# In-projection by rows: one pinned weight split instead of many, and a unit's first sums in the quarter before

## The chip, the cores and the metric

The kernel runs on one core of a Trainium2 chip. The metric is the device time of one execution in microseconds (us). The core's engines are PE (TensorE: matmuls, and the weight loads PEld that overlap them), ACT (ScalarE), DVE (VectorE), POOL (GpSimd) and SP (SyncE, which here issues the DMAs). Each engine works through its own instruction queue in order; semaphores order the queues against each other.

## The reference

The reference is one inference step of a two-layer backbone, for 128 context tokens and 128 latent tokens with a model width of 2048. Layer 0 mixes with MLA and grouped-query attention in parallel, layer 1 with differential attention; each layer ends in a gated feed-forward block with a convolution. What matters here is the start of layer 0:

```python
mod = jax.nn.silu(cond) @ w_ada[l] + b_ada[l]
sh1, sc1, gt1, sh2, sc2, gt2 = jnp.split(mod[:, None, :], 6, axis=-1)
h = rmsnorm(x, g_norm_mix[l]) * (1 + sc1) + sh1
...
proj = h @ w_in
```

So before the first projection can start on a block of 128 input features, the shift `sh1` and the scale `sc1` of these features have to be computed from `w_ada`, 2048 rows each. `w_in` is 2048 by 2880.

## The kernel before

**Precision.** A product of two float32 matrices is made from three matmuls in a faster format. Every weight tile is split into a high part `wh` and a low part `wl` (`split`, L225 to L227: ACT copies the tile with rounding, DVE subtracts), the activations `hx` likewise, and a product is `wh*hx_hi + wh*hx_lo + wl*hx_hi`. A DMA brings 16 blocks of 128 by 128 weights (1 MB) into a buffer `raw` (three buffers); a split takes 8 of these blocks, and `wh` and `wl` have four buffers each.

**The in-projection by rows** (`mixer_ab`). Tokens lie on the free axis: all 256 tokens (128 of each group) are one moving operand. There are 16 input blocks k and 23 output columns c. The projection goes in four quarters of four input blocks, so that it can begin when the first block's shift and scale are known. In a quarter the first ten columns ("held", `HELD`) stay in five PSUM banks while the input blocks come one after another (quarter 0: four slices of one block each) or two and two (quarters 1 to 3: two slices); then the other 13 columns follow with all four blocks of the quarter at once (the "free" columns c10 to c22). The result of each quarter is added into SBUF (`leave`).

**The units** (`Early`) give shift and scale. Units 0 to 3 are one input block each, units 4 to 9 two blocks each. A unit has two sums over its weights (`sums(1)` for the scale, from `araw` buffers; `sums(0)` for the shift, from `condb`), 32 small matmuls each, into one PSUM bank `ada`. Then `turn` copies the bank to SBUF on ACT (`am`, L422), `finish` transposes it on PE (L429) and adds up on DVE (L432 to L437), and `modulate` makes the block's `hx` (DVE L589 and L597, ACT L600 and L601, and L584 for the low half, on DVE for even and POOL for odd blocks). `end` is `finish` and `modulate` together. In quarter 0 units 1 to 3 come between the held products; unit 2q+4 comes in the free columns of quarter q, for the first slice of the next quarter, and unit 2q+3 in the first slice of quarter q (1 to 3), for its second slice.

**What sets the order.** The program is planned at compile time: each engine's queue is filled by a planner that takes, by its own estimate of durations, what is ready, earlier traced work first. `keep_in_program_order` pins an instruction behind the one traced before it on its engine. The matmuls of the in-projection are pinned (`product`, until the middle of quarter 3), the sums and transposes of the units too, and in quarter 0 the DMA issues and, through `W.pinned`, the two instructions of each weight split. `W` is a `Stream`: `block` hands out the blocks one by one, and when it has none left it makes the next split from the oldest `raw`. Quarter 0 takes 92 blocks: 40 in the held slices, that is splits 1 to 5, and 52 in the free columns. `W.pinned = False` stands behind the last held slice.

Of the kernel before, what the change touches and what calls it, by code (L numbers as in the profile page):

```python
# [88 lines left out]
def step_kernel(ctx: ExitStack, tc: tile.TileContext, A: dict):  # L89
# [22 lines left out]
    def T_(pl, shape, tag, dt=F32, bufs=None):  # L112
        kw = {} if bufs is None else {"bufs": bufs}
        return pl.tile(shape, dt, tag=tag, name=nm(tag), **kw)
# [84 lines left out]
    def att_bank():  # L199
        return T_(ppool["att"], [P, 512], "att", bufs=3)  # L200
# [24 lines left out]
    def split(out_hi, out_lo, src, pin=lambda i: i):  # L225
        pin(act.copy(out_hi, src))  # L226
        pin(dve.tensor_tensor(out=out_lo, in0=src, in1=out_hi.bitcast(F32), op=ALU.subtract))  # L227
# [72 lines left out]
    class Stream:  # L300
# [15 lines left out]
        def block(self):  # L316
            if not self.blocks:
                if not self.raws:
                    self.fetch()
                raw, n = self.raws[0]  # L320
                m = min(8, n - self.lo)
                wh = T_(wpool, [P, 1024 + P], "wh", F32R, bufs=4)[:, :m * P]
                wl = T_(wpool, [P, 1024 + P], "wl", F32R, bufs=4)[:, :m * P]
                split(wh, wl, raw[:, self.lo * P:(self.lo + m) * P],
                      tc.keep_in_program_order if self.pinned else lambda i: i)
                self.blocks = [(wh[:, b * P:(b + 1) * P], wl[:, b * P:(b + 1) * P]) for b in range(m)]
                self.lo += m
                if self.lo == n:
                    self.raws.pop(0)
                    self.lo = 0  # L330
            return self.blocks.pop(0)
# [146 lines left out]
    def load_row():  # L478
        tc.keep_in_program_order(sp.dma_start(out=condb, in_=A["condb"]))
        for r in range(2):  # L480
            tc.keep_in_program_order(act.activation(condb[:, r], condb[:, r], AF.Silu))
# [237 lines left out]
    def mixer_ab(hx, W, units, st):  # L719
        l = 0  # L720
        with tc.tile_pool(name="ab", bufs=1) as ab:
            with tc.tile_pool(name="abp", bufs=1) as pj:
# [9 lines left out]
                def caches():  # L732
                    tc.keep_in_program_order(sp.dma_start(out=ckc, in_=A["cache_ckv"]))
                    split(kv_in[:, :, 0, T:2 * T], kv_in[:, :, 1, T:2 * T], ckc)
                    for i, half in enumerate(halves):
                        tc.keep_in_program_order(sp.dma_start(out=kr[half, i, T:2 * T], in_=A["cache_krope"][half]))
                    tc.keep_in_program_order(sp.dma_start(out=kg[:, :, T:2 * T], in_=A["cache_gqa_k"]))
                    tc.keep_in_program_order(sp.dma_start(out=vg[:, 1], in_=A["cache_gqa_v"]))
# [81 lines left out]
                def finish(c):  # L820
                    if c < 6:
                        start(queries(c))
                    elif c < 10:
                        start(latents(c - 6))
                    elif c == 10:
                        start(key_rope())
                    elif c < 13:
                        start(keys(c - 11))
                    elif c == 14:
                        start(values(0))  # L830
                    elif c == 15:
                        start(values(1))
# [22 lines left out]
                def product(ps, c, ks, first, last):  # L855
                    pin = (lambda i: i) if free[0] else tc.keep_in_program_order
                    for k in ks:
                        wh, wl = W.block()
                        for n, (w, lo) in enumerate(((wh, 0), (wh, NT), (wl, 0))):
                            pin(pe.matmul(ps, w, hx[:, k, lo:lo + NT], start=first and k == ks[0] and n == 0,  # L860
                                          stop=last and k == ks[-1] and n == 2, skip_group_check=True))

                def leave(c, n, ps, q):
                    to = pr[:, c:c + n] if c < 15 else qb[:, c - 15:c - 15 + n]
                    if q == 0:
                        act.copy(to, ps)
                    else:
                        dve.tensor_tensor(out=to, in0=to, in1=ps, op=ALU.add)

                def held(banks_, ks, q, between, last=False):  # L870
                    first = ks[0] % 4 == 0
                    for c in range(HELD):
                        product(banks_[c // 2][:, c % 2 * NT:(c % 2 + 1) * NT], c, ks, first and c % 2 == 0, last)
                        if last and c % 2:
                            leave(c - 1, 2, banks_[c // 2].rearrange("p (c t) -> p c t", c=2), q)
                            if q == 3:
                                finish(c - 1)
                                finish(c)
                        between(c)

                def at(**steps):
                    return lambda c: [f() for f in steps.get(f"c{c}", ())]

                def scale(u):
                    modulate(hx, rb0, 0, 0, range(u.c0, u.c0 + u.n), held=0 < u.c0 < 4)

                def end(u):
                    u.finish()
                    scale(u)

                scale(units[0])
                for q in range(4):
                    banks_ = [T_(pacc, [P, 512], "acc") for _ in range(3)] + [att_bank() for _ in range(2)]
                    if q == 0:
                        u1, u2, u3 = units[1:4]
                        pin = tc.keep_in_program_order

                        def load(u):
                            u.load(1, pin)
                            u.load(0, pin)  # L900

                        load(u2)
                        u1.sums(1)
                        held(banks_, [0], 0, at(c1=[lambda: u1.sums(0), u1.turn, lambda: load(u3)], c4=[lambda: end(u1)]))
                        W.fetch(pin)
                        u2.sums(1)
                        held(banks_, [1], 0, at(c4=[lambda: u2.sums(0), u2.turn], c6=[lambda: end(u2)]))
                        W.fetch(pin)
                        u3.sums(1)
                        u3.sums(0)  # L910
                        u3.turn()
                        held(banks_, [2], 0, at(c2=[lambda: end(u3)]))
                        held(banks_, [3], 0, at(), True)
                        W.pinned = False
                    else:
                        u = units[2 * q + 3]
                        ks = range(4 * q, 4 * q + 4)
                        held(banks_, ks[:2], q, at(c0=[lambda: u.sums(1)], c2=[lambda: u.sums(0), u.turn],
                                                   c3=[lambda: end(u)]))
                        if q == 3:  # L920
                            free[0] = True
                            pinned[0] = True
                            caches()
                            load_row()
                        held(banks_, ks[2:], q, lambda c: pump(RATE["in3"]) if q == 3 else None, True)
                    if q < 3:
                        u = units[2 * q + 4]
                        u.load(1)
                        u.load(0)
                        steps = at(c13=[lambda: u.sums(1)], c16=[lambda: u.sums(0), u.turn], c17=[lambda: end(u)],  # L930
                                   c18=[lambda: [units[2 * q + 5].load(j) for j in (1, 0)]])
                    else:
                        steps = lambda c: pump(RATE["in3"])
                    for c in range(HELD, NIN):
                        ps = T_(pacc, [P, 512], "acc")[:, :NT]
                        product(ps, c, range(4 * q, 4 * q + 4), True, True)
                        leave(c, 1, ps[:, None, :], q)
                        if q == 3:
                            finish(c)
                        steps(c)  # L940
# [77 lines left out]
        with tc.tile_pool(name="abo", bufs=1) as feat["pool"]:  # L1018
            ensure(l, 2)
            ada["pew"] = PEW["out0"]  # L1020
            W = Weights(A["w_out_ab"], KD, 1)
# [195 lines left out]
    with banks("pab") as ppool["ada"]:  # L1217
# [3 lines left out]
        units = [Early(k, 1) for k in range(4)] + [Early(c, 2) for c in range(4, KD, 2)]  # L1221
        W = Stream(A["w_in_ab"], ([TB] * 5 + [12]) * 4)
# [7 lines left out]
        W = Weights(A["w_up"][0], KD, 1)  # L1230
# [5 lines left out]
    with tc.tile_pool(name="cc", bufs=1) as cp, banks("pc") as ppool["ada"]:  # L1236
        ada["junk"] = lambda: T_(cp, [P, 4, 512], "junk", BF16, bufs=1)
        ppool["att"] = ppool["ada"]
        W = Weights(A["w_in_c"], KD, 1)
# [5 lines left out]
        W = Weights(A["w_up"][1], KD, 1)  # L1245
# [154 lines left out]
```

## Time and profile before

| | before |
|---|---|
| median of 3 runs | 2341.72 us (2340.18 to 2345.34) |
| the profiled execution | 2342.78 us, span 2341.0 us |
| mean granted clock of PE | 0.989 |
| PE busy | 2282.4 us (97%) |
| DVE busy | 1817.4 us (78%) |
| ACT busy | 1178.3 us (50%) |
| first held product starts, first free column starts, quarter 1 starts | 22.0, 63.9 and about 86.5 us |

The span runs from the first to the last instruction; the execution's own time lies 1.8 us around it. PE's busy share counts matmuls at whatever clock was granted, so a matmul at half clock counts double. A row of a timeline gives start, duration, engine, line, operation, what is written from what, the shape, how many instructions are merged, and in brackets the idle time of the engine before it and what ended that. A row of DMA issues ends in the time from issue to landing.

### The profile page before, as it was taken

The page shows a single profiled execution, that of the slowest core. Times are in us where ns is not written, and L with a number is a line of the kernel's source. Part 1 is how long each engine was busy: PE and PEld are TensorE (multiplying, and loading weights), DVE is VectorE, ACT ScalarE, POOL GpSimd, SP SyncE. Part 2 cuts the span into 40 slices and gives each one's busy share as a digit, 9 for nine tenths or more (in the row PEclk, how much of TensorE's full clock was granted, in tenths as well). Part 3 has the DMA queues.
Part 4 walks back from the last instruction along what each step waited for, and adds up shares of the span by engine and source line. Part 5 has one row for each costly group of instructions (what it writes and reads, how often), then busy time and mean ns, then how long its engine had stood idle before and what let it go on. Part 6 is the DMA issues. An engine that isn't in the chain of part 4 may idle for free. (4 is left out here: it accounts for less than half of the span.)

```text
span 2341.0 us, 47384 instructions
## 1 busy us (share of the span) xinstructions
PE 2282.4 (97%) x19806; PEld 2191.6 (94%) x19806; DVE 1817.4 (78%) x2636; ACT 1178.3 (50%) x1865; POOL 149.5 (6%) x133
## 2 busy tenths in 40 slices
PE   5999999999999999999999999999999999999998
PEld 4888878899999999999989999898999999999997
DVE  3566748879999999999969989787899755666654
ACT  2446664465553345554465555446555434555553
POOL 0002101200000000001220000022000000000011
PEclk8999999999999999999999999999999999999999
DMA  8797779867777877777767788786677555555553
GB/s 353 304 359 284 256 294 378 313 255 252 260 263 285 309 263 257 261 264 270 293 237 265 268 325 292 294 317 234 229 260 268 198 196 189 194 197 198 189 192 126
DMA packets 92566, 610.82 MB, mean 261 GB/s; under 512 B 9984, under 2 KB 17856, under 8 KB 20544
## 3 DMA queue, kind: packets, MB, share of 16 engines
q1 hardware_dynamic: 92352, 607.80, 70.5%
q8 instruction: 155, 2.54, 0.4%
q14 instruction: 59, 0.48, 0.1%
HBM read 603.01 MB, written 4.75 MB: 260 GB/s over the span
## 5 line engine op out<-in xcount | busy, mean ns | idle before, releaser
L226 ACT CAST wh<-raw 128x1024 fp32r<-128x1024 f32 (+1 forms) x788 | 792.8, 1012 | 883.2 <-PE acc L377 688.5
L227 DVE TENSOR_TENSOR wl<-raw,wh 128x1024 fp32r<-128x1024 f32 (+1 forms) x788 | 922.6, 1186 | 316.6 <-ACT wh L226 308.4
L376 PE MATMUL acc<-hx,wh 128*128 128x256 f32 x3440 | 952.5, 277 | 1.4 <-ACT wh L226 0.8
L380 PE MATMUL acc<-hx,wl 128*128 128x256 f32 x3440 | 951.5, 277 | 0.2 <-DVE wl L227 0.2
L377 PE MATMUL acc<-hx,wh 128*128 128x256 f32 x3440 | 951.4, 277 | 0.0
L376 PEld LDWEIGHTS acc<-hx,wh 128*128 128x128 f32 x3440 | 646.0, 188 | 7.8 <-issue 5.0
L380 PEld LDWEIGHTS acc<-hx,wl 128*128 128x128 f32 x3440 | 645.6, 188 | 6.4 <-issue 4.2
L377 PEld LDWEIGHTS acc<-hx,wh 128*128 128x128 f32 x3440 | 646.0, 188 | 1.9 <-issue 1.7
L486 DVE CUSTOM_DVE_ANT_0 junk<-araw,condb 128x2048 f32<-128x2048 f32 (+1 forms) x192 | 443.5, 2310 | 0.0
L377 PE MATMUL acc<-g,wh 128*128 128x256 f32 x1408 | 388.3, 276 | 0.0
L380 PE MATMUL acc<-g,wl 128*128 128x256 f32 x1408 | 388.0, 276 | 0.0
L376 PE MATMUL acc<-g,wh 128*128 128x256 f32 x1408 | 387.8, 276 | 0.0
L377 PEld LDWEIGHTS acc<-g,wh 128*128 128x128 f32 x1408 | 264.3, 188 | 0.0
L380 PEld LDWEIGHTS acc<-g,wl 128*128 128x128 f32 x1408 | 264.2, 188 | 0.0
L376 PEld LDWEIGHTS acc<-g,wh 128*128 128x128 f32 x1408 | 264.1, 188 | 0.0
L181 POOL TENSOR_TENSOR sqacc<-sqacc,sq 128x256 f32<-128x256 f32 x62 | 86.2, 1390 | 1576.1 <-issue 1300.0
L860 PE MATMUL acc<-hx,wh 128*128 128x256 f32 x608 | 115.4, 290 | 7.9 <-ACT wh L226 5.6
L860 PEld LDWEIGHTS acc<-hx,wh 128*128 128x128 f32 x608 | 95.6, 194 | 16.3 <-ACT wh L226 6.4
L1169 ACT ACTIVATE cv<-acc,convw 128x256 f32<-128x256 f32 x176 | 98.3, 559 | 1.4 <-PE acc L364 1.4
L650 DVE SCALAR_TENSOR_TENSOR x<-acc,mod,x 128x128 f32<-128x128 f32 x192 | 58.0, 343 | 41.0 <-PE acc L380 40.0
L860 PE MATMUL acc<-hx,wl 128*128 128x256 f32 x304 | 86.7, 286 | 2.2 <-DVE wl L227 2.2
L1172 DVE SCALAR_TENSOR_TENSOR cv<-acc,convw,cv 128x254 f32<-128x254 f32 x176 | 83.7, 476 | 4.8 <-ACT cv L1169 4.8
(253 smaller groups left out, 2490.0 us busy)
## 6 DMA issues: line engine op xcount, KB each, us to landing
raw<-w_up SPq DMA_DIRECT2D x176, 1024.0 KB, 4.8
araw<-w_ada SPq DMA_DIRECT2D x160, 1024.0 KB, 5.3
raw<-w_down SPq DMA_DIRECT2D x88, 1024.0 KB, 4.8
raw<-w_in_c SPq DMA_DIRECT2D x48, 1024.0 KB, 5.6
raw<-w_in_ab SPq DMA_DIRECT2D x20, 1024.0 KB, 7.3
araw<-w_first SPq DMA_DIRECT2D x16, 1024.0 KB, 9.2
condb<-w_first SPq DMA_DIRECT2D x16, 1024.0 KB, 10.9
raw<-w_out_ab SPq DMA_DIRECT2D x16, 1024.0 KB, 7.8
```

What stands on the lines that cost most here:

```text
L181: pool.tensor_tensor(out=st["acc"], in0=st["acc"], in1=sq, op=ALU.add)
L226: pin(act.copy(out_hi, src))
L227: pin(dve.tensor_tensor(out=out_lo, in0=src, in1=out_hi.bitcast(F32), op=ALU.subtract))
L376: fixed(pe.matmul(ps[:, :n], wh, xh(k), start=(i == 0), stop=False))
L377: fixed(pe.matmul(ps[:, :n], wh, xl(k), start=False, stop=False))
L380: fixed(pe.matmul(ps[:, :n], wl, xh(k), start=False, stop=(i == last)))
L486: tc.keep_in_program_order(dve.tensor_tensor_reduce(out=junk, in0=raw, in1=condb[:, c].rearrange("p (g n) -> p g n", g=4), scale=1.0, scal ...
L650: dve.scalar_tensor_tensor(out=x[:, c, s], in0=ps[:, s], scalar=mod[:, l, 3 * which + 2, c, g:g + 1], in1=x[:, c, s], op0=ALU.mult, op1=AL ...
L860: pin(pe.matmul(ps, w, hx[:, k, lo:lo + NT], start=first and k == ks[0] and n == 0, stop=last and k == ks[-1] and n == 2, skip_group_check ...
L1169: pin(act.activation(y, ps, AF.Identity, scale=cw[:, 1, m:m + 1], bias=cw[:, 3, m:m + 1]))
L1172: pin(dve.scalar_tensor_tensor(out=y3[:, :, 1:], in0=p3[:, :, :T - 1], scalar=cw[:, 0, m:m + 1], in1=y3[:, :, 1:], op0=ALU.mult, op1=ALU.add))
```

## The change

Two edits. `Stream.block` clears `self.pinned` after its first split, so that only that one is pinned, and the line that cleared it after the held slices of quarter 0 is gone. And for the units that serve the second slice of quarters 1 to 3, `sums(1)` moves from behind column 0 of the first slice to behind column 21 of the preceding quarter, `sums(0)` and `turn` from behind column 2 to behind column 0, and `end` from behind column 3 to behind column 2.

```diff
                 split(wh, wl, raw[:, self.lo * P:(self.lo + m) * P],
                       tc.keep_in_program_order if self.pinned else lambda i: i)
+                self.pinned = False
...
                         held(banks_, [3], 0, at(), True)
-                        W.pinned = False
                     else:
                         u = units[2 * q + 3]
                         ks = range(4 * q, 4 * q + 4)
-                        held(banks_, ks[:2], q, at(c0=[lambda: u.sums(1)], c2=[lambda: u.sums(0), u.turn],
-                                                   c3=[lambda: end(u)]))
+                        held(banks_, ks[:2], q, at(c0=[lambda: u.sums(0), u.turn], c2=[lambda: end(u)]))
...
                         steps = at(c13=[lambda: u.sums(1)], c16=[lambda: u.sums(0), u.turn], c17=[lambda: end(u)],
-                                   c18=[lambda: [units[2 * q + 5].load(j) for j in (1, 0)]])
+                                   c18=[lambda: [units[2 * q + 5].load(j) for j in (1, 0)]],
+                                   c21=[lambda: units[2 * q + 5].sums(1)])
```

## Prediction

> **What bounds the kernel now.** I read the page first, then who PE waited for in the first 230 us, then the span in steps of the granted clock, then the timelines of ACT, PE and SP there.
>
> ```profile
> PE 2282.4 (97%) x19806; PEld 2191.6 (94%) x19806; DVE 1817.4 (78%) x2636; ACT 1178.3 (50%) x1865; POOL 149.5 (6%) x133
> ...
> PE acc L860 <- ACT wh L226: 5.6, 3, 3.3
> PE att L860 <- ACT wh L226: 2.7, 2, 1.9
> PE acc L860 <- POOL hx L584: 2.3, 2, 1.2
> PE acc L860 <- DVE wl L227: 2.2, 3, 1.0
> PE att L860 <- DVE wl L227: 1.5, 2, 0.8
> ...
> 30.04:33.45 3.41, 1.94 (x30) 1.61 (x34) 1.23 (x1) 0.66 (x1) 0.52 (x1) 0.97 1.01 420
> 33.45:36.86 3.41, 3.41 (x29) 3.03 (x22) 0.00 (x0) 0.00 (x0) 0.00 (x0) 0.53 1.02 423
> ...
> 47.10:50.52 3.42, 0.50 (x2) 0.30 (x2) 2.09 (x6) 1.69 (x3) 0.73 (x1) 0.97 0.93 376
> 50.52:53.93 3.41, 2.83 (x13) 2.83 (x14) 0.53 (x1) 0.00 (x0) 0.00 (x0) 0.50 0.51 173
> 53.93:57.34 3.41, 2.24 (x11) 1.94 (x10) 0.00 (x0) 1.14 (x2) 0.00 (x0) 0.50 0.37 151
> 57.34:60.76 3.42, 2.51 (x10) 2.21 (x11) 2.99 (x3) 3.42 (x5) 0.00 (x0) 0.50 0.00 0
> 60.76:64.17 3.41, 3.41 (x19) 3.41 (x19) 1.64 (x2) 1.71 (x4) 0.00 (x0) 0.53 0.83 264
> ```
>
> PE is busy 97% of the span, so a microsecond that PE loses early in the span is a microsecond of the end. The waits (total, times, longest) show PE losing 5.6 + 2.7 + 2.2 + 1.5 = 12.0 us to weight splits; all ten lie before 60 us, in the held products of the first quarter. The windows (stretch, PE, PEld, DVE, ACT, POOL busy, granted clock, DMA share, GB/s) show a second loss: after a stretch with 1.47 us or more of PE idle the clock is granted at half, once for 3.4 us and then for 13.7 us, until a stretch without idle (60.76) ends it. ACT and DVE are mostly idle there: the splits are late for want of order, not of engine time.
>
> ```profile
> 38.33 0.37 ACT L422 COPY am<-ada 128x256 f32<-128x256 f32 x1 [7.64 <-PE ada L414]
> 38.60 1.05 ACT L226 CAST wh<-raw 128x1024 fp32r<-128x1024 f32 x1
> ...
> 56.20 0.59 ACT L866 COPY proj<-acc 128x512 f32<-128x512 f32 x1 [6.61 <-PE acc L860]
> 56.69 3.88 ACT L226 CAST wh<-raw 128x1024 fp32r<-128x1024 f32 x4
> ...
> 7.55 0.33 SPq L312 DMA_DIRECT2D raw<-w_in_ab  x1
> ...
> raw<-w_in_ab SPq DMA_DIRECT2D x1, 1024.0 KB, 19.0
> ...
> 26.82 5.49 SPq L312 DMA_DIRECT2D raw<-w_in_ab  x2
> ...
> raw<-w_in_ab SPq DMA_DIRECT2D x1, 1024.0 KB, 12.2
> ```
>
> The pin is what holds them. The third split reads a raw tile issued at 7.55 that landed 19.0 us later, at 26.6, yet it started at 38.60, behind the copy of unit 2's sums, which waited 7.64 us for PE. The fifth reads the tile issued at 26.82, landed at 39.0, and started at 56.69, behind a PSUM copy that waited 6.61 us for PE. So PE waits for a cast that queues behind a copy that waits for PE.
>
> **The change part by part.** No instruction and no byte is added or removed. (a) Splits 2 to 10 of the first quarter lose their pins; splits of later quarters had none. (b) In quarters 1 to 3 the 32 loads and 32 matmuls of a unit's first sums move ahead of two products, into the end of the quarter before; its second sums, its copy and its `end` come two products and one product earlier.
>
> Part (a), its most. The first split stays pinned; PE waits 0.67 us for it (the row at 22.03 below) and about as much for its low half, so 12.0 - 1.4 = 10.6 us of waits can go. Of the half-clock stretches half of PE's busy time goes: (3.41 + 2.83 + 2.24 + 2.51 + 3.41) / 2 = 7.2 us. Together 17.8 us.
>
> Part (a), by the path that remains. Other waits can step in: the landing of the unit loads, and the chain transposes, sums, scale, hx.
>
> ```profile
> 22.03 0.50 PE L860 MATMUL acc<-hx,wh 128*128 128x256 f32 x2 [0.67 <-ACT wh L226]
> 28.61 0.28 PE L860 MATMUL att<-hx,wl 128*128 128x256 f32 x1
> ...
> 41.19 0.38 PE L429 MATMUL att<-cst,am 128*128 128x128 f32 x2
> 42.54 1.08 PE L414 MATMUL ada<-araw,condw 128*32 128x128 f32 x32
> 63.91 0.42 PE L860 MATMUL acc<-hx,wh 128*128 128x256 f32 x2
> 64.29 0.39 PE L860 MATMUL acc<-hx,wh 128*128 128x256 f32 x2
> 64.63 0.39 PE L860 MATMUL acc<-hx,wh 128*128 128x256 f32 x2
> ...
> 29.83 0.74 POOL L584 TENSOR_TENSOR hx<-nt,hx 128x256 fp32r<-128x256 f32 x1 [12.83 <-ACT hx L601]
> 43.50 0.42 DVE L584 TENSOR_TENSOR hx<-nt,hx 128x256 fp32r<-128x256 f32 x1 [0.61 <-ACT hx L601]
> ...
> 14.78 0.33 SPq L405 DMA_DIRECT2D araw<-w_first  x1
> ...
> araw<-w_first SPq DMA_DIRECT2D x1, 1024.0 KB, 14.3
> ...
> 26.44 0.33 SPq L405 DMA_DIRECT2D condb<-w_first  x1
> ...
> condb<-w_first SPq DMA_DIRECT2D x1, 1024.0 KB, 10.1
> ```
>
> One block of a held product takes 64.63 - 64.29 = 0.34 us at full clock, one unit's sums 1.1 us, with 0.2 us to change over. Column 7 of the first slice ends at 28.9; columns 8 and 9 no longer wait: 29.6. Unit 2's first tile landed at 14.78 + 14.3 = 29.1: sums to 30.9. Slice 1 needs hx of unit 1, whose low half ends at 30.6: five columns to 32.7, second sums to 34.0, two columns, transposes (0.38) and three columns to 36.1. Unit 3's sums, whose last tile lands at 26.44 + 10.1 = 36.5, end at 38.5. Unit 2's hx is ready 43.92 - 41.57 = 2.35 us after its transposes (35.1), so at 37.5: no wait. Slice 2: three columns to 39.6, transposes to 40.0, seven to 42.4. Unit 3's hx is ready 2.35 to 2.7 us after 40.0 (its low half is POOL's, 0.74 for 0.42): 42.4 to 42.7. The fifth split (raw at 39.0, cast 1.05, subtraction 1.23) is ready at 41.3. Slice 3 ends at 42.7 + 10 x 0.34 + 0.6 = 46.7, counting 0.6 for changes. The first free column started at 63.91: 17 us earlier at best. The whole backlog of loads before the next weight tile is five tiles more at the 2.5 us that separate the landings at 36.5 and 39.0, about 51.5, and that tile's first block is due six columns of 4 x 0.34 and one set of sums later, at 56: it holds.
>
> What can be given back is order: a free split can sit in front of the chain.
>
> ```profile
> 454.68 1.98 ACT L226 CAST wh<-raw 128x1024 fp32r<-128x1024 f32 x2
> ...
> 458.17 0.61 PE L362 MATMUL acc<-hx,wh 128*128 128x256 f32 x3 [1.40 <-ACT hx L601]
> ...
> 97.97 1.23 DVE L227 TENSOR_TENSOR wl<-raw,wh 128x1024 fp32r<-128x1024 f32 x1
> 98.32 1.46 POOL L584 TENSOR_TENSOR hx<-nt,hx 128x256 fp32r<-128x256 f32 x1 [14.91 <-ACT hx L601]
> ```
>
> At 454.68 two unpinned casts went ahead of hx casts and PE then waited 1.40 us for hx. At 97.97 an unpinned subtraction ran beside POOL's low half, which took 1.46 us for the usual 0.74. Per unit I bound this by 0 and 1.4 us plus 0.7: up to 2.1, for three units 6.3. I take 1 us each, between the ends, since the rows show about one such event a unit, of 0.7 to 1.4; so 17 - 3 = 14.
>
> Part (b). PE waits for POOL's hx twice, 2.3 us in all (the wait row), once in each of quarters 1 and 2: after 98.32 + 1.46 = 99.8 in the first. The chain starts one product of two blocks earlier against the second slice: 2 x 0.34 = 0.7 us each, bounded by 0 (the split again beside POOL) and 1.2: I take 1.4 for both. PE's work is only reordered. The moved sums read two tiles whose loads go out once the previous unit's first sums free the buffers, eight free columns (8 x 4 x 0.34 = 11 us) and that unit's second sums (2) before the new place. The loads quoted took 10.1 to 14.3 us in the worst backlog; with the queue shorter I take no wait, at the outside 1.3 us for each of three units, and behind that wait only products are queued on PE. The PSUM bank was copied out five columns before. Two loads on SP that need those buffers go out some 2 us earlier, past weight tiles that are issued well ahead of need: nothing, and 1 us if one is pushed back.
>
> Sum: 14 + 1.4 = 15.4 us, 2342.8 - 15.4 = 2327.4 for the profiled execution, which lies 1.1 us over the median of the runs shown: **2326.3** against 2341.7.
>
> The Trainium skill (TensorE: Matmul & The Clock Gate, Part 1) has the clock fall to half after an idle window of about 3.4 us and return after one busy window. The trace differs: 1.47 us of idle within 3.41 was enough, and 0.58 us (50.52) already kept it low. By the page nothing on the new path could halve the clock; by the rows it could, and the rows decide.
>
> **The rivals.** *ACT blocked by a landing.* The order on ACT is planned ahead, so a cast planned for a tile that lands later stops everything behind it.
>
> ```profile
> 160.25 0.62 ACT L226 CAST kv_in<-ckc 128x512 fp32r<-128x512 f32 x1 [4.23 <-DMA ckc<-cache_ckv]
> 17.95 0.37 ACT L422 COPY am<-ada 128x256 f32<-128x256 f32 x1 [6.70 <-PE ada L414]
> ```
>
> That has happened at 160.25. If the fifth split stands before unit 2's copy, the copy comes at 39.0 + 1.05 = 40.1 instead of 34.0: 6 us of the 14 go, 2332.3. Against it: loads in the first 40 us are slow because they queue, which a planner may well count. *The clock stays low.* Slices 1 to 3 at half clock are 30 blocks that take up to 0.34 us longer, 10 us, less some 3 that hide behind landings: 2333. The short gaps left (under 1 us) speak against it. *No change.* If the planner thinks tiles land late, casts keep their places and only (b) stays: 2340. *Slower.* The second to fourth splits are planned before unit 0's copy (17.95). The second raw tile lands at 26.6, two casts end at 28.7, the copy is 10.7 us late and so is unit 1's last sum; SP issues the third tile behind a load that waits for it, 26.82 becomes 37.5, landing at 49.7 if it takes 12.2 again. With the fifth split ahead of unit 2's copy, slice 1 goes on at 51 instead of 41; the remaining 11.6 us lead to 62.7, at half clock some 5 more: 67.7, 4 us late, less 1.4: 2344.3. It decides from a block of 17 us in all; ACT's idle 6.70 us before that copy leaves the room.
>
> **How the numbers follow.** Forecast 0.64, blocked ACT 0.14, low clock 0.08, no change 0.06, slower 0.08. A measurement of this kernel tells 0.2% (4.7 us) from no change, so the first three are faster: 0.86. The low end is all 17.8 + 2.3 us: 2321.6, rounded to 2321; the high end is blocked ACT and a low clock partly together, 10 us given back: 2336.
>
> **What would show it.** In the profile after: casts of splits 2 to 5 at about 22, 27, 28 and 39 instead of 29.66, 38.60, 48.56 and 56.69; PE's waits on wh and wl in this stage down from 12.0 to about 1.4; full clock from 27 to 64; the first free column near 50 (46.7 plus 3) instead of 63.9; waits on POOL's hx of 0.5 us or none in quarters 1 and 2. Wrong it is if ACT shows a long wait on a raw landing before 45 with an am copy behind it, or if the first column is early but the end is not.

## The result, and the profile after

The changed kernel takes 2329.35 us (median of 4 runs, 2326.71 to 2332.07) against 2342.01 for the kernel before beside it: a ratio of 0.9944 with a 95% interval of 0.9927 to 0.9962. It is faster, by 12.7 us in the medians; the forecast was 2326.3 with a range of 2321 to 2336. The profiled execution took 2326.71 us (span 2324.9) against 2342.78 (span 2341.0), 16.1 us less. Two more sets of five runs of the same kernel gave 2329.22 against 2343.43 and 2329.60 against 2342.42, so the gain in medians is 12.7, 14.2 and 12.8 us, and the profiled execution flatters it.

The page of the changed kernel, and who PE waited for in its first 230 us (total, times, longest):

```profile
PE 2275.1 (98%) x19806; PEld 2185.2 (94%) x19806; DVE 1819.8 (78%) x2636; ACT 1177.9 (51%) x1865; POOL 145.9 (6%) x133
...
PE acc L861 <- ACT hx L602: 1.5, 1, 1.5
PE acc L861 <- POOL hx L585: 1.1, 2, 0.8
PE att L430 <- ACT am L423: 1.1, 1, 1.1
...
PE acc L861 <- DVE wl L227: 0.8, 1, 0.8
PE acc L861 <- ACT wh L226: 0.7, 1, 0.7
```

The 12.0 us of waits for `wh` and `wl` are down to 0.8 + 0.7 = 1.5, both of the first split. New are 1.5 us for an `hx` of ACT and 1.1 for an `am` copy. (Line numbers are one higher than before, by the added line.)

The windows of the same kernel (stretch, then PE, PEld, DVE, ACT, POOL busy, granted clock, DMA share, GB/s):

```profile
43.35:46.76 3.41, 1.39 (x8) 1.19 (x9) 3.41 (x5) 0.63 (x2) 1.15 (x1) 0.96 1.00 411
46.76:50.17 3.41, 3.41 (x19) 3.41 (x18) 1.58 (x3) 2.38 (x4) 0.00 (x0) 0.54 1.02 423
...
65.97:106.68 40.71, 40.71 (x414) 36.48 (x413) 24.24 (x40) 17.85 (x28) 1.50 (x2) 1.00 0.89 353
```

One window at half clock (46.76) is left between 27 and 64 us, where there were 3.4 and 13.7 us. The last row goes from the transposes of unit 4 to those of unit 6, the length of one quarter: 414 matmuls in 40.71 us, PE without a gap. The same work in the kernel before, where PE is idle for 1.16 us:

```profile
79.14:121.83 42.69, 41.53 (x414) 36.99 (x413) 24.66 (x40) 17.84 (x28) 2.21 (x2) 1.00 0.89 344
```

Where the time went is best seen from marks that are the same work in both programs: the transposes of units 4, 6 and 8, which stand behind column 17 of quarters 0, 1 and 2; the last residual `x` of the out-projection; the first `cv` of the feed-forward block. (The second row of each fence is unit 5, whose place the change moves; it is used further down.) The timelines of PE, DVE and ACT, first of before, then of after (start, duration; unit 6 is the end of the two windows above):

```profile
79.14 0.60 PE L429 MATMUL att<-cst,am 128*128 128x128 f32 x4
93.31 0.63 PE L429 MATMUL att<-cst,am 128*128 128x128 f32 x4
164.51 0.60 PE L429 MATMUL att<-cst,am 128*128 128x128 f32 x4
449.54 0.61 DVE L650 SCALAR_TENSOR_TENSOR x<-acc,mod,x 128x128 f32<-128x128 f32 x2 [1.80 <-PE acc L380]
475.06 0.56 ACT L1169 ACTIVATE cv<-acc,convw 128x256 f32<-128x256 f32 x1
```

```profile
65.97 0.60 PE L430 MATMUL att<-cst,am 128*128 128x128 f32 x4
79.48 0.60 PE L430 MATMUL att<-cst,am 128*128 128x128 f32 x4
147.40 0.60 PE L430 MATMUL att<-cst,am 128*128 128x128 f32 x4
431.11 0.61 DVE L651 SCALAR_TENSOR_TENSOR x<-acc,mod,x 128x128 f32<-128x128 f32 x2 [1.82 <-PE acc L381]
460.07 0.56 ACT L1169 ACTIVATE cv<-acc,convw 128x256 f32<-128x256 f32 x1
```

The first free column starts at 50.79 us instead of 63.91. At unit 4 the changed kernel is 13.2 us ahead, at unit 6 15.15, at unit 8 17.1. So the first quarter brings 13.2, and each of the next two brings 1.97 more (121.83 - 79.14 = 42.69 against 40.71 us). From the last `x` to the first `cv` it takes 28.35 us (460.07 - 431.72) where it took 24.9 (475.06 - 450.15), and some of the lead is lost there. The same marks of all profiled executions, in us:

| kernel | unit 4 | unit 6 | unit 8 | last x ends | first cv | span |
|---|---|---|---|---|---|---|
| before | 79.14 | 121.83 | 164.51 | 450.15 | 475.06 | 2341.0 |
| after | 65.97 | 106.68 | 147.40 | 431.72 | 460.07 | 2324.9 |
| again (after) | 66.10 | 106.81 | 147.52 | 433.09 | 462.29 | 2327.4 |
| again2 (after) | 66.04 | 106.75 | 147.46 | 433.51 | 462.54 | 2327.8 |
| a_only | 66.03 | 108.59 | 151.26 | 438.27 | 462.33 | 2329.9 |
| b_only | 79.50 | 120.21 | 160.92 | 441.36 | 466.11 | 2333.2 |
| first_free | 66.45 | 107.16 | 147.88 | 433.52 | 463.13 | 2331.6 |
| warm | 71.62 | 114.30 | 156.66 | 442.22 | 466.25 | 2337.4 |
| fix_u1 | 63.14 | 103.85 | 144.56 | 430.28 | 459.30 | 2323.4 |
| fix_u3 | 63.02 | 103.93 | 144.64 | 425.29 | 454.36 | 2320.1 |
| fix_u3b (fix_u3) | 64.50 | 105.21 | 145.92 | 432.34 | 461.99 | 2324.8 |
| fix_all | 62.46 | 103.17 | 143.88 | 430.59 | 459.95 | 2324.5 |
| cure | 66.21 | 107.11 | 147.83 | 436.44 | 461.24 | 2329.5 |
| cure_u3 | 63.31 | 104.02 | 144.74 | 430.07 | 456.60 | 2322.5 |

Up to unit 8 the three executions of the changed kernel agree within 0.15 us; the two of `fix_u3` differ by 1.5 from the start on. Between unit 8 and the last `x` executions of one program differ by up to 5.8 us, as the section on the hardware shows, so single spans are read with care.

### The profile page after: what moved, and what is told of

Read it like the earlier page. It is cut to its first block, busy times and chain, and to the rows that moved or that the text cites. A ratio compares the mean times of both kernels' runs of the same rounds, so it can differ in the third digit from the quotient of the medians.

```text
span 2324.9 us, 47382 instructions
## 1 busy us (share of the span) xinstructions
PE 2275.1 (98%) x19806; PEld 2185.2 (94%) x19806; DVE 1819.8 (78%) x2636; ACT 1177.9 (51%) x1865; POOL 145.9 (6%) x133
## 5 line engine op out<-in xcount | busy, mean ns | idle before, releaser
L861 PEld LDWEIGHTS acc<-hx,wh 128*128 128x128 f32 x608 | 93.4, 190 | 10.9 <-issue 5.7
L651 DVE SCALAR_TENSOR_TENSOR x<-acc,mod,x 128x128 f32<-128x128 f32 x192 | 57.9, 343 | 40.8 <-PE acc L381 39.8
```

The lines of the kernel that those rows point to most:

```text
L651: dve.scalar_tensor_tensor(out=x[:, c, s], in0=ps[:, s], scalar=mod[:, l, 3 * which + 2, c, g:g + 1], in1=x[:, c, s], op0=ALU.mult, op1=AL ...
```

## Experiments

Every ratio below is that of the runs to runs of the kernel before on the same chip, with its 95% interval.

### The two parts alone

First the changed kernel again, beside the two halves of the change.

> The changed kernel itself, timed once more beside the kernel before, as the mark for the other runs. Theory (the forecast's: late splits and the half clock behind them, 13 us, and POOL's hx in quarters 1 and 2, 2 to 3 us): a ratio of 0.9935 to 0.995, the first free column 13 us earlier than before. Rival (a reshuffled plan that happens to be good in one program): the same program, so the same time; it tells nothing between them by itself.

Measured: 2329.22 us, 0.9941 (0.9929 to 0.9953).

`a_only` keeps the free splits and puts sums and `end` back:

```diff
-                        held(banks_, ks[:2], q, at(c0=[lambda: u.sums(0), u.turn], c2=[lambda: end(u)]))
+                        held(banks_, ks[:2], q, at(c0=[lambda: u.sums(1)], c2=[lambda: u.sums(0), u.turn],
+                                                   c3=[lambda: end(u)]))
...
-                                   c18=[lambda: [units[2 * q + 5].load(j) for j in (1, 0)]],
-                                   c21=[lambda: units[2 * q + 5].sums(1)])
+                                   c18=[lambda: [units[2 * q + 5].load(j) for j in (1, 0)]])
```

> Only the pins go; the sums stay in their old places. Theory: the first free column starts at 51 us as in the changed kernel (63.9 before), PE's two waits of 1.16 us for POOL's hx at the second slices of quarters 1 and 2 stay, and the time is 11 to 14 us under before (ratio about 0.9945 to 0.9953). Rival 1 (the moved sums carry the gain): under 4 us. Rival 2 (the gain is chance of the plan): anywhere between 0 and 16.

Measured: 2332.56 us, 0.9952 (0.9940 to 0.9964).

`b_only` keeps the moved sums and pins all the splits of the held slices:

```diff
-                self.pinned = False
...
                         held(banks_, [3], 0, at(), True)
+                        W.pinned = False
```

> Only the sums move; the splits of quarter 0 stay pinned. Theory: the first free column stays at 63.9 us, the two waits of 1.16 us go, 2 to 4 us under before by the end of quarter 3 and in the time. Rival 1: most of the 13 us. Rival 3 (the half clock comes from the units' sums and not from late splits): the half-clock stretch of 13.7 us goes here too.

Measured: 2337.31 us, 0.9978 (0.9969 to 0.9987). That is 6.1 us in medians where 2 to 4 were expected; at unit 8 `b_only` is 3.6 us ahead, as expected. What the medians hold beyond that isn't explained; in its profile the stretch behind unit 8 ran without a window at half clock (last section).

The parts add up where they work. At unit 4 `a_only` is 13.1 us ahead of before (79.14 - 66.03) and keeps the old quarters (42.56 and 42.67 us); `b_only` is not ahead there but has the short quarters, 40.71 twice, so 3.94 us for the two. 13.2 + 3.94 = 17.1, which is what the changed kernel has at unit 8. Rows of quarter 1 show (b) at work, unit 5's chain on DVE before the change, then POOL's low half after it:

```profile
94.47 1.23 DVE L227 TENSOR_TENSOR wl<-raw,wh 128x1024 fp32r<-128x1024 f32 x1
95.62 0.15 DVE L437 SCALAR_TENSOR_TENSOR scl<-mod,cst 128x4 f32<-128x4 f32 x1
```

```profile
83.22 0.75 POOL L585 TENSOR_TENSOR hx<-nt,hx 128x256 fp32r<-128x256 f32 x1 [12.97 <-ACT hx L602]
```

Before, one subtraction of a split (94.47) stands on DVE inside the chain, behind the op at 94.20, and holds up the scale by 1.2 us, and a second (97.97) runs beside POOL's low half, which takes 1.46 us. `a_only`, which has the old places, has both as well (81.37 on DVE; POOL 1.47 at 85.41). With the sums moved, the scale follows at once (80.34, then 80.55), no subtraction runs beside POOL's op, and that op takes half the time. The whole chain from the transposes to the end of that op was 6.5 us before (93.31 to 99.78) and is 4.5 now (79.48 to 83.97; both transposes are unit 5's rows above). In `a_only` PE still waits four times for POOL's `hx` in the first 230 us, 3.4 us in all; in `b_only` not once, while its waits for splits are those of before.

At the end of the program, in medians, `a_only` brings 10.9 us, `b_only` 6.1, and both 14.2, less than their sum of 17.0. Each of these has an interval of 2 to 3 us to either side, so the times alone don't show that the parts fail to add. The last experiment looks at the stage where the profiles differ.

### Was the first split's pin needed?

`first_free` is the changed kernel with `self.pinned = False` from the start, so the first split is left to the planner too.

> The changed kernel with the first split unpinned too. Theory of the slower rival (a cast planned for a tile that has not landed stops ACT's queue): if the planner believes the first weight tile lands before unit 0's copy at 17.7, the first casts stand in front of it, wait for the landing at 17.6, and everything from the first product on comes 1 to 2 us later. Rival (the planner knows the landings well): no difference from the changed kernel, within 1 us at the first free column.

Measured: 2331.43 us, 0.9946 (0.9934 to 0.9958). The timelines of ACT and PE of `first_free`:

```profile
18.63 1.99 ACT L226 CAST wh<-raw 128x1024 fp32r<-128x1024 f32 x2
...
23.09 0.40 ACT L602 CAST hx<-nt 128x256 fp32r<-128x256 f32 x1
...
23.55 1.04 PE L861 MATMUL acc<-hx,wh 128*128 128x256 f32 x2 [1.77 <-ACT hx L602]
```

The planner puts two casts behind unit 0's copy (18.36) and ahead of its `hx` cast, which comes at 23.09 instead of 20.40 (the changed kernel's ACT rows, below). PE waits 1.77 us for it, but at the first free column (51.27) and at unit 4 only 0.5 us of that is left (66.45 for 65.97). No cast was put in front of the copy, so the slower rival's order didn't come about even without any pin. By these marks the pin of the first split is worth half a microsecond; the times (2331.43 and 2329.22) can't tell that from nothing.

### Waits or clock?

`warm` is the kernel before with 60 matmuls of no use in PE's waits of the held slices; they go to an unused half of a PSUM bank, so the output stays the same and PE only has more to do.

```diff
+                fill = {(0, 8): (14, 1), (1, 6): (6, 2), (2, 4): (27, 3), (3, 2): (13, 3)}
...
+                        if (ks[0], c) in fill:
+                            n_, u_ = fill[ks[0], c]
+                            for _ in range(n_):
+                                tc.keep_in_program_order(pe.matmul(
+                                    units[u_].ps[:, 256:512], hx[:, 0, :P], hx[:, 0, :NT], start=True, stop=True,
+                                    skip_group_check=True))
```

> The kernel before, with 14, 6, 27 and 13 matmuls more (128 by 256, into columns of unit 1's to 3's PSUM bank that nothing reads) in front of the four held products at which PE waits for a pinned split. They fill PE's waits of 1.86, 0.89, 3.33 and 1.62 us without shortening them and keep PE busy; nothing else changes. Theory (the half clock is a loss of its own, some 5 to 7 us of the 13): the half-clock stretches at 33.5 and from 50.5 to 64.2 us go, and the first free column starts at 57 to 59 us instead of 63.9; the time falls by 4 to 7 us. Rival (only the waits count, the half clock hides in them): the first free column stays within 1 us of 63.9.

Measured: 2335.58 us, 0.9971 (0.9961 to 0.9981), 6.4 us less by doing more. Three windows of `warm`:

```profile
23.21:26.62 3.41, 3.41 (x51) 3.08 (x52) 0.17 (x1) 0.37 (x1) 0.00 (x0) 1.00 1.01 413
33.45:36.86 3.41, 3.41 (x49) 2.77 (x48) 0.23 (x1) 1.32 (x2) 0.00 (x0) 1.00 1.01 413
50.52:64.17 13.65, 12.82 (x123) 11.37 (x122) 8.21 (x7) 10.55 (x16) 0.00 (x0) 1.00 0.60 218
```

The start of the first free column in its PE timeline:

```profile
56.44 0.39 PE L860 MATMUL acc<-hx,wh 128*128 128x256 f32 x2
```

Both half-clock stretches are gone, and the free column starts at 56.44 instead of 63.91, 7.5 us earlier, with every split still queued behind the same op of ACT as before. (The casts come earlier too, 28.19, 35.55, 45.52 and 51.46 for splits 2 to 5, since what these ops wait for comes sooner.) But not all of this is the added matmuls' doing. They start at 27.27, and the profile before has one more window at half clock ahead of that:

```profile
23.21:26.62 3.41, 3.33 (x38) 2.63 (x39) 0.03 (x1) 0.17 (x1) 0.00 (x0) 0.53 1.01 411
```

`warm` was at full clock there (the first of the three rows) and stood 1.45 us ahead just before its first added matmul (27.16 for 28.61). The changed kernel was at half clock in that window too (0.59), so it is no part of what the change brings. That leaves 6.0 us for the two stretches that the filling removes: of the 13 us of part (a) some 6 are the clock and the rest the waits themselves, and a reading by waits alone falls.

### What the planner's order gives back in the first quarter

The changed kernel's ACT timeline, and the rows of unit 3's chain on DVE and PE:

```profile
20.40 0.40 ACT L602 CAST hx<-nt 128x256 fp32r<-128x256 f32 x1
20.71 1.99 ACT L226 CAST wh<-raw 128x1024 fp32r<-128x1024 f32 x2
26.17 1.99 ACT L226 CAST wh<-raw 128x1024 fp32r<-128x1024 f32 x2 [3.48 <-DMA raw<-w_in_ab]
28.07 0.36 ACT L423 COPY am<-ada 128x256 f32<-128x256 f32 x1
...
39.54 2.00 ACT L226 CAST wh<-raw 128x1024 fp32r<-128x1024 f32 x2
...
44.08 0.41 ACT L602 CAST hx<-nt 128x256 fp32r<-128x256 f32 x1 [1.00 <-DVE nt L598]
...
41.19 1.40 DVE L590 TENSOR_TENSOR nt<-x,misc 128x256 f32<-128x256 f32 x4
42.52 1.22 DVE L227 TENSOR_TENSOR wl<-raw,wh 128x1024 fp32r<-128x1024 f32 x1
43.65 0.34 DVE L598 TENSOR_SCALAR nt<-nt,scl,mod 128x128 f32<-128x128 f32 x1
...
44.54 0.39 PE L861 MATMUL acc<-hx,wh 128*128 128x256 f32 x1 [1.47 <-ACT hx L602]
45.76 0.39 PE L861 MATMUL acc<-hx,wh 128*128 128x256 f32 x1 [0.84 <-POOL hx L585]
```

At 26.17 two casts wait for the landing of the second `raw` tile and unit 1's copy stands behind them: PE's wait of 1.1 us for `am`. At 41.19 the first products of later units (x4 for the one that unit 3 needs) and a subtraction go ahead of unit 3's scaling at 43.65: PE loses 1.47 + 0.84 us, and the window of these waits (43.35, with 2.02 us of idle) is followed by one at half clock.

The `fix` kernels are the changed one with a split's planned place behind a given instruction. In `split`'s caller:

```diff
+        def behind(self, n):
+            return hxmade[3] if n in (5, 6, 7) else ()
...
+                self.made = getattr(self, "made", 0) + 1
+                with ExitStack() as es:
+                    for i in self.behind(self.made):
+                        es.enter_context(tc.issue_after(i.ins))
+                    split(wh, wl, raw[:, self.lo * P:(self.lo + m) * P],
+                          tc.keep_in_program_order if self.pinned else lambda i: i)
```

This is `fix_u3`; `fix_u1` has `hxmade[1] if n in (3, 4)` instead. `hxmade[c]` is the `hx` cast and the DVE scaling of input block c. `fix_u3` holds the first products of the later units (L590) behind unit 3's scaling too; `fix_all` does both, with the low halves of blocks 1 and 3 on DVE.

> The changed kernel, with splits 3 and 4 queued behind the hx cast of unit 1 on ACT and behind its scaling on DVE. Theory (free casts that wait 3.5 us for the landing at 26.4 held up unit 1's copy): the copy comes at 26.4 us instead of 28.1, PE's wait of 1.1 us at the transposes at 28.7 goes, and the first free column starts 0.5 to 1 us earlier than at 51.0. Rival (the landing of unit 2's and 3's loads is what binds there): no change at slice 2, 39.4 us.

> The changed kernel, with splits 5 to 7 and the products with x of the later units (L590) queued behind unit 3's hx cast on ACT and its scaling on DVE. Theory (free splits in front of unit 3's chain cost the waits of 1.47 and 0.84 us at 44.8 and 46.0 and the half-clock stretch after them): slice 3 starts at 43.2 to 43.6 us instead of 44.8, no half clock at 46.8, the first free column at 47 to 48.5 us instead of 51.0. Rival (the fifth split is then late in its turn and PE waits for it at column 2): 50 us or more.

> Both orders together, and the low halves of units 1 and 3 on DVE (0.42 us) instead of POOL (0.73 to 1.15 us). Theory: the first free column at 46.5 to 47.5 us, 3.5 to 4.5 us earlier than in the changed kernel, and the time 3 to 5 us lower, near 2325. Rival (clock and plan of the later stages move by as much): the column early, but the time within 2 us of the changed kernel's 2329.2.

Measured: `fix_u1` 2325.31 us, 0.9926 (0.9913 to 0.9938); `fix_u3` 2326.00, 0.9926 (0.9915 to 0.9938); `fix_all` 2326.21, 0.9930 (0.9917 to 0.9942). The timelines of ACT and PE in `fix_u3`:

```profile
42.15 0.41 ACT L614 CAST hx<-nt 128x256 fp32r<-128x256 f32 x1
42.47 3.88 ACT L226 CAST wh<-raw 128x1024 fp32r<-128x1024 f32 x4
...
47.72 0.40 PE L875 MATMUL acc<-hx,wh 128*128 128x256 f32 x2
```

Among PE's waits in the first 230 us ACT's `hx` has no row any more, and POOL's has 0.6 us. The `hx` cast now stands ahead of the casts of splits, the free column starts at 47.72 instead of 50.79, and no window in slice 3 is at half clock. That is 3.1 us at the free column and 2.9 at unit 4. `fix_u1` reaches nearly the same marks (47.95 and 63.14), more than the 0.5 to 1 us expected, but there the planner also changed its order at unit 3, so the run doesn't tell what unit 1's copy costs by itself. Both together bring little more than either: 47.28 and 62.46.

Since the gain is about what these runs can just tell, `fix_u3` was run once more with the changed kernel beside it.

> The changed kernel beside the reordered one on the same chip. Theory: about 2329, a ratio to before of 0.994.

> The kernel of fix_u3 once more (splits 5 to 7 and the later units' products behind unit 3's chain), on the same chip as the changed kernel. Theory: 3 us lower than the changed kernel, a ratio to before of 0.9925 to 0.993, the first free column at 48 us. Rival (the difference between fix_u3 and the changed kernel was one of chips and calls): within 1 us of the changed kernel.

Measured: changed kernel 2329.60 us, 0.9944 (0.9931 to 0.9956); `fix_u3` 2326.57, 0.9934 (0.9920 to 0.9947). On one chip that is 3.0 us less, and the intervals overlap. In this pair of profiles `fix_u3` is only 1.5 us ahead at unit 4. Both start slice 2 at 40.8 us; the changed kernel starts slice 3 at 46.22 and `fix_u3` at 44.56, 1.7 us earlier as in the first pair (44.54 and 42.88). What is missing is the half clock behind the wait: the changed kernel's slice 3 took 4.63 us this time and 6.25 in its first profile. So unit 3's order is worth 1.7 us, and about 1.4 more when half clock follows. In this pair PE waited 2.8 and 2.2 us for unit 1's `am` copy, which casts waiting for their tile held up, where it was 1.1 in the first profile. The landing differs between executions, and this edit doesn't touch that loss. The marks show a gain in both; the total makes it likely, not certain.

### What is given back later

From the last `x` to the first `cv` the kernels without both parts (before, `a_only`, `b_only`, `warm`) take 24.0 to 24.9 us, and the eight profiles with both parts, the two `cure` kernels aside, 28.4 to 29.7. Every queue is planned by the planner's estimates from the start, and with both parts it arrives at the feed-forward block with another order. From the last `x` to the end of the span before takes 1890.9 us, `a_only` 1891.7, `b_only` 1891.9, and the changed kernel 1893.2, 1894.4 and 1894.3 in its three profiles. That looks like 2.3 to 3.5 us lost, but it isn't shown: `warm`, which has neither part and the short stretch, takes 1895.2 us, and the two executions of `fix_u3` differ by 2.4. The changed kernel's timelines of POOL, DVE and PE there:

```profile
434.41 1.63 POOL L193 TENSOR_TENSOR rr<-rv,cst 128x2 f32<-128x2 f32 x1 [6.44 <-DVE rv L189]
...
434.25 1.23 DVE L227 TENSOR_TENSOR wl<-raw,wh 128x1024 fp32r<-128x1024 f32 x1
...
438.93 1.22 DVE L227 TENSOR_TENSOR wl<-raw,wh 128x1024 fp32r<-128x1024 f32 x1
...
436.61 0.70 PE L221 MATMUL att<-diag,cst 128*128 128x256 f32 x2 [1.87 <-DVE diag L213]
439.80 0.61 PE L363 MATMUL acc<-hx,wh 128*128 128x256 f32 x3 [1.50 <-ACT hx L602]
442.85 0.58 PE L364 MATMUL acc<-hx,wh 128*128 128x256 f32 x1 [2.44 <-DVE hx L585]
```

A subtraction of a split runs right behind `rv` and beside POOL's root, which takes 1.63 us. In before that subtraction stood ahead of `rv`, and the root took 0.70 (timeline of POOL):

```profile
451.82 0.70 POOL L193 TENSOR_TENSOR rr<-rv,cst 128x2 f32<-128x2 f32 x1 [5.40 <-DVE rv L189]
```

From `rv` to the first low half of `hx` on DVE three subtractions stand in DVE's queue instead of two, and it takes 8.2 us instead of 7.1. PE waits 5.8 us in this stretch instead of 3.8. So 2.0 of the 3.4 us are waits; the other 1.4 are PE busy (22.54 us for 171 matmuls, before 21.15 for 158), work that before does outside the stretch and that isn't lost. `cure` puts the order back: two splits ahead of the statistics, two behind the fourth first product.

```diff
+        if not fixed:
+            raws_ = [W.load(), W.load()]
+            early = (raws_, {(c, 0): W.halves(raws_[c], 0) for c in range(2)})
+            with tc.issue_after(W.low.ins):
+                r = stat_rstd(st, D, att_bank)
...
+                with ExitStack() as es:
+                    if early:
+                        es.enter_context(tc.issue_after(fourth[0].ins))
+                    blocks[c, h] = W.halves(raws[c], 8 * h)
```

> The changed kernel with the order of one later stage, the one ahead of feed-forward 0, put back as before: the first two weight splits of that stage stand ahead of the statistics on DVE (before they did, in the changed kernel the second stands beside POOL's root), and the next two behind the fourth nt product. Only the order of instructions differs; nothing in the in-projection is touched. Theory (the new plan there gives back 3 to 4 us of what the in-projection gains): POOL's root op back to 0.70 us from 1.63, PE's wait for diag down from 1.9 to about 1.0 (a group of row sums still stands between the statistics matmuls, 1.06 us), from the last x to the first cv 26 to 27.5 us instead of 28.4 to 29.2, and 1 to 3 us off the time: about 2327. Rival (that stage is longer only because more of the row sums lies in it, and nothing is lost): the stage gets shorter by under 1 us and the time stays at 2329.3.

> Both orders together: the splits of the in-projection behind unit 3's chain (3 us found), and the later stage's splits as before. Theory: 2326.3 less 1 to 3, about 2324. Rival: 2326.3, as without the second edit.

Measured: `cure` 2328.07 us, 0.9935 (0.9921 to 0.9948); `cure_u3` 2327.25, 0.9936 (0.9922 to 0.9949). POOL's root in `cure`:

```profile
439.29 0.70 POOL L193 TENSOR_TENSOR rr<-rv,cst 128x2 f32<-128x2 f32 x1 [6.59 <-DVE rv L189]
```

And PE's waits of `cure` in that stretch:

```profile
PE misc L520 <- DMA araw<-w_ada: 2.9, 2, 2.4
PE att L221 <- DVE diag L213: 1.1, 1, 1.1
```

The root is back at 0.70, the wait for `diag` at 1.1, the waits for `hx` are gone, and the stretch to the first `cv` is 24.8 us (`cure_u3`: 26.5) instead of 28.4 to 29.2. So the order made those waits. But a wait of 2.9 us for a load takes their place, and from the last `x` to the end `cure` takes 1893.1 us, 0.1 to 1.3 less than the changed kernel, and `cure_u3` 1892.4 against 1894.8 and 1892.4 in the two profiles of `fix_u3`. In the times nothing of it can be told from no gain: 1.3 us under the changed kernel, and none on top of `fix_u3`. So the expected 1 to 3 us are not shown. The waits of this stretch are explained; whether the total loses anything by them is open. Between these kernels the clearest gain is `fix_u3`'s, 2326.0 and 2326.6 us in two sets.

## Why the prediction was right, and where it wasn't

**The pins.** Right in mechanism and nearly in size: 14 us forecast, 13.2 measured at unit 4 and 13.1 in `a_only`. The casts of splits 2 to 5 were to come at about 22, 27, 28 and 39; they came in the pairs that start at 20.71, 26.17 and 39.54. The free column was to be near 50 and starts at 50.79. The path without order losses, 46.7, is not far from what `fix_u3` reaches, 47.72.

**The clock.** 7.2 of the 17.8 us of "its most" were put down to half clock, and `warm` found 6.0 from these stretches alone. The prediction counted two half-clock stretches; the profile has a third before them (23.21, above), which stays after the change and so costs the forecast nothing. Its rule of 1.47 us of idle and more fits these stretches, but not all of the profile (last section). But "full clock from 27 to 64" failed: one stretch remains, behind a wait that the order made.

**Order losses.** Three of 1 us each were allowed for. They are there, as PE waits of 1.1 (unit 1's copy), 1.47 and 0.84 (unit 3), plus 1.7 us of half clock behind the last in the first profile, which one execution of three didn't have. The first is the rival of ACT blocked by a landing, in small: casts planned for a tile that landed late, a copy behind them, but 1 us and not 6, since the fifth split was not put ahead of unit 2's copy. The row it was foreseen from, a cast that had waited for its tile, was the right one to look at.

**The moved sums.** This step failed in size: 1.4 us forecast, 3.9 measured, outside its bounds of 0 to 2.3. It was worked out as a chain that starts one product earlier. What the runs show is a chain that is itself 2.0 us shorter: 1.2 us because no subtraction stands inside it on DVE any more, 0.7 because none runs beside POOL's low half. The prediction had the second, 1.46 us beside the split, and kept it only as a bound; the first, at 94.47, it did not see. That the planner places the subtractions so well is an outcome of its order and was not worked out ahead. Of the 1.97 us per quarter the wait on POOL's `hx` is 1.4: the matmul behind it starts 1.54 us after the one ahead of it (98.29 to 99.83) where the usual step is 0.11. The profile's 1.16 leaves out the end of the record ahead. For the other half microsecond, the products behind the wait follow each other a little more slowly before (0.35 us a block for 0.34, from 100.17 on); why wasn't tested. The quarter's waits on POOL's `hx` are gone, as was said; the loads of the moved sums cost nothing, as was said.

**What no step had.** The sum was 15.4 and the lead at unit 8 is 17.1. The prediction took everything behind the in-projection to be shifted whole. It isn't: the stretch ahead of the first `cv`, some 285 us after unit 8, has another order and is 3.4 to 4.3 us longer, 2.0 of them waits in the profile after. The lead in medians is 12.7 to 14.2 us. So the moved sums brought 2.5 us more than forecast and the pins 0.8 less, and 3 to 4 us of the lead at unit 8 don't show at the end; part of that is the changed order, the rest can't be told from the scatter. That the number is near is partly luck; that the kernel is faster, and why, is not.

**Rivals.** No change falls by the casts' times. A low clock throughout falls by the windows. The slower case, with splits ahead of unit 0's copy, did not come about even in `first_free`.

## What to carry to other kernels

A pin that orders a producer behind a copy that waits for the producer's consumer costs twice here: the wait, and the half clock that can follow it. Price both, from the windows of the granted clock and not from the wait list alone. When a planner is given back its freedom, hold the one short chain that PE will wait for next ahead of the free work (here 1.5 to 3 us by holding three splits and the products of later units), and compare every later stage, since a plan can change far from the edit. Look too for the first point where two profiles part: in `warm` 1.45 of the 7.5 us were there before the first added matmul ran.

## What the runs showed of the hardware

**The clock.** In the changed kernel a window with 2.02 us of idle in 3.41 (43.35, above) was followed by half clock; in the profile before 1.47 was enough. A window with 1.10 us of idle in 3.42 was not followed by one, in the changed kernel:

```profile
26.62:30.04 3.42, 2.32 (x21) 2.12 (x20) 2.72 (x6) 1.82 (x3) 0.00 (x0) 1.00 1.01 419
```

In the profile before, once low it stayed low through windows with gaps (50.52 to 60.76); here it came back after one without any (46.76, above: PE busy for all of it). But idle time in the window alone doesn't decide, as two windows of the profile before show:

```profile
234.84:238.26 3.42, 3.42 (x15) 1.74 (x16) 1.60 (x8) 3.40 (x10) 0.83 (x2) 0.50 0.48 141
453.30:456.71 3.41, 1.93 (x14) 0.74 (x13) 2.88 (x11) 2.43 (x4) 0.00 (x0) 1.00 0.96 382
```

The first has no idle at half clock, and the next window was still at half; the second has 1.48 us of idle, and the next was at full clock (0.97). And the same waits (1.5 and 0.84 us, ahead of and in slice 3) were followed by half clock in two profiles of the changed kernel and not in the third, `again2`. What else counts these runs don't show. The Trainium skill (TensorE: Matmul & The Clock Gate, Part 1) puts the fall after an idle window of about 3.4 us; no single wait in these rows is that long (the longest is 3.3, on ACT's `wh` before), so the measurement decides here. Its other half, that one busy window brings the clock back, agrees with the windows at 46.76 and 60.76 and not with the one at 234.84.

**Executions of one program differ by the clock.** `fix_u3` and `fix_u3b` are one program. From unit 8 to the last `x`, first the one, then the other:

```profile
144.64:425.29 280.65, 275.54 (x2252) 236.23 (x2250) 206.18 (x398) 153.41 (x324) 34.17 (x34) 1.00 0.83 316
```

```profile
145.92:432.34 286.42, 281.34 (x2252) 239.20 (x2250) 206.34 (x398) 153.94 (x324) 34.18 (x34) 0.98 0.81 310
```

The same 2252 matmuls with the same idle time (280.65 - 275.54 = 5.1 us, 286.42 - 281.34 = 5.1) took 5.8 us longer, at a mean granted clock of 0.98 instead of 1.00. `b_only`, at 1.00 too, took 280.4 us for them; the executions with windows at half clock in this stretch took 284.3 to 288.6. Which short gaps fall into one window decides it, it seems; that was not tested. It is why single spans scatter by 5 us here, and part of why the first profile's 16.1 us was flattering.

**A small op on POOL beside a large one on DVE.** POOL's root on two columns took 1.63 us beside a subtraction on DVE and 0.70 without it; the low half 1.46 and 0.75. In both cases POOL's op ended a little after the subtraction, by 0.56 us (436.04 for 435.48) and 0.58 (99.78 for 99.20). The Trainium skill (SBUF — State Buffer, SBUF: two separate sides) has DVE with two SBUF inputs and a GpSimd op that reads SBUF share a pair of ports as an exclusive lock; these rows agree.
